# First layer of a two-layer encoder: a written TensorE order in small pieces, and softmax steps queued further back

## The chip, the cores and the metric

The kernel runs on one core of one Trainium2 chip. TensorE (PE) multiplies matrices into PSUM, VectorE (DVE) and ScalarE (ACT) read PSUM and SBUF, GpSimd (POOL) reads and writes SBUF alone, SyncE (SP) issues the DMAs. Each engine takes its instructions in their order; semaphores hold an instruction until what it reads is there. The metric is the device time of one execution in microseconds (us), lower is better.

## The reference, cut to what matters

1024 frames of a new stream and 32 frames of a running one go through two layers. Layer 0, the one that is changed, projects its normed input to u, q, k, v and two gates, and has two branches: trailing means of u over windows of 2, 4, 8 and 16 frames, mixed by a matrix per group (four groups of 128 channels), and attention of 8 heads over the frame's own chunk of 64 and the 8 before it.

```python
def even_mixer(h, w_in, w_mix, scale, table, w_out, pool_hist=None, k_hist=None, v_hist=None):
    proj = h @ w_in
    u, q, k, v, g_pool, g_att = jnp.split(proj, [P, P + A, P + 2 * A, P + 3 * A, 2 * P + 3 * A], axis=-1)
    ...
        pool_out = multi_scale_pool(u, 0, 0, w_mix, scale)
        att = band_attention_prompt(q, k, v, table)
    ...
    mixed = jnp.concatenate([pool_out * jax.nn.silu(g_pool),
                             att.reshape(B, L, A) * jax.nn.silu(g_att)], axis=-1)
    return mixed @ w_out, new_pool, new_k, new_v
```

In the attention, `s` is q times k plus a bias by distance, `p = softmax(s)`, and the output `p` times v. The 32 frames of the running stream ("the sample") attend to 512 cached rows and themselves. Layer 1 is not touched.

## The kernel before, in words

The 1056 tokens stand in the columns of all tiles, in three groups of 384, 384 and 288 (`GR`). A dense pass (`dense`, `mm3`) multiplies one 128-column block of a weight with the whole input: 8 slices of the input dimension, three products each (high by high part, low by high, high by low: L106, L107, L108) into a PSUM tile pd (three of them), which DVE or ACT empties (`scaled` L256, `gated` L268 and L271, u L612). A weight comes in two halves: SP loads wr, ACT rounds it to wh (L93), POOL subtracts to get wl (L94, "the split").

The loop goes over four pairs of heads. A pair has the dense passes K and GA (the gate, in the one tile ga), the attention of its two heads, and between its parts the passes of `PLAN`: v and q of the next pair, u and gp of a group of channels. Attention runs in two halves of 512 queries: scores in banks of PSUM (ps, three tiles), L342 and L343; bias and copy to SBUF tiles st (DVE L347, ACT L355, and a corner cleared by POOL, L359); maxima over the keys (DVE `mx` L371, then POOL's all-reduce over partitions `mb`, L373); subtraction (DVE L377), exponential (ACT L378); the product with the values, PV (L388); at the end of a half `att_out`: POOL multiplies by the gate (L408), DVE forms a reciprocal (L409) and multiplies (L410). There is one tile each of ro, rg and mb.

The sample has scores of its own (L429, L430) with a small all-reduce `smb` (L441) and an exponential (L444), its ten products with the values (L454), reciprocal and scaling (L456, L457) and a transpose back (L459). `pool_sums` forms the trailing sums of u: one sum on POOL (L477) per doubling of the window, four for group 3 down to one for group 0, then DVE corrects the first frames (L481) and updates u (L483). `pool_mix` multiplies by the group's matrix (PE L495) into one PSUM tile pm, which DVE empties (L497). After the loop `out_proj` reads what was stored, and POOL and DVE split it (L196).

Tile's scheduler orders all engines; the source order only ranks them.

Of the kernel before, what the change touches and what calls it, by code (L numbers as in the profile page):

```python
# [7 lines left out]
F32 = mybir.dt.float32  # L8
# [7 lines left out]
DEC = 32  # L16
# [17 lines left out]
class Net:  # L34
# [5 lines left out]
    # ---------------------------------------------------------------- consts  # L40
    def consts(self):
# [4 lines left out]
        # the table of the activations, before the data is there  # L46
# [24 lines left out]
    # keeps [s, t] with s <= t  # L71
# [4 lines left out]
    # ---------------------------------------------------------------- dense  # L76
# [40 lines left out]
    # the same, one token group at a time, to be put between other work; "make" gives evac when the tile starts  # L117
    def later(self, take, xs, make, after=None):
        box = {}

        def step(gi):
            if gi == 0:
                box["w"] = take()
                box["ev"] = make()
# [3 lines left out]
        self.fills += [lambda gi=gi: step(gi) for gi in range(3)]  # L128
# [15 lines left out]
    # r = 1/sqrt(sum/1024 + eps), on all partitions, from per-partition sums; worked out with the tokens on the partitions  # L144
# [44 lines left out]
    # split x * g into two parts of 12 bits  # L189
# [15 lines left out]
    # the input: one group's tokens, with tiles that are not in use yet for what comes in  # L205
# [23 lines left out]
    # ---------------------------------------------------------------- layer 0  # L229
# [21 lines left out]
    def scaled(self, dst, sc=None):  # L251
        nc, r = self.nc, self.r0

        def ev(gi, s, n, p):
            if sc is None:
                nc.vector.tensor_tensor(out=dst[:, s:s + n], in0=p[:, :n], in1=r[:, s:s + n], op=ALU.mult)  # L256
            else:
                nc.vector.scalar_tensor_tensor(out=dst[:, s:s + n], in0=p[:, :n], scalar=sc, in1=r[:, s:s + n],
                                               op0=ALU.mult, op1=ALU.mult)
        return ev  # L260

    # (1 + tanh(g/2)) * g, twice the silu
    def gated(self, dst):
        nc, r = self.nc, self.r0

        def ev(gi, s, n, p):
# [4 lines left out]
            nc.vector.scalar_tensor_tensor(out=d, in0=th[:, :n], scalar=1.0, in1=d, op0=ALU.add, op1=ALU.mult)  # L271
        return ev

    def v_tokens(self, vT, pr):
# [8 lines left out]
        for b0 in (0, 4, 8):  # L283
            p = self.pv.tile([128, 512], F32, name="pv") if b0 == 4 else self.pm.tile([128, 512], F32, name="pm")
            for b in range(b0, min(b0 + 4, NCH)):
                L = clen(b)
                q = p[:L, (b - b0) * 128:(b - b0) * 128 + 128]
                nc.tensor.transpose(q, vT[:, 128 * b:128 * b + L], self.ident)
                nc.scalar.mul(out=v4[:L, b, 0::2, :], in_=q.rearrange("p (t c) -> p t c", c=64), mul=self.rcol[:L, b:b + 1])
        for e in range(2):  # L290
            c0 = pr * 128 + e * 64
            cs = slice(e * 128, e * 128 + 64)
            nc.sync.dma_start(out=io["vo"][0:512, c0:c0 + 64].rearrange("(b p) c -> p b c", p=128), in_=vt[:, 4:8, cs])
            nc.sync.dma_start(out=io["vo"][512:544, c0:c0 + 64], in_=vt[:DEC, 8, cs])
        return vt

    # hi and lo of both heads, stacked on the partitions
# [21 lines left out]

    def att_s(self, pr, e, hf, Q, KA, KB, B):  # L320
# [7 lines left out]
        for group in banks:  # L328
            st = self.lp.tile([128, 1280], F32, name="st", bufs=4)
            tiles.append((st, [j for js in group for j in js]))  # L330
            off = 0
            for js in group:
# [3 lines left out]
                for j in js:  # L336
                    a, b = max(128 * j, q0), min(128 * j + 640, q1)
                    n = b - a
                    dst = st[:, off + w:off + w + n]
# [884 lines left out]
```

## Time and profile before

| | us |
|---|---|
| median of 3 runs | 1275.29 |
| the runs | 1273.09, 1277.02, 1275.29 |
| span of the profiled execution | 1273.6 |
| PE busy | 1200.1 (94%) |
| DVE busy | 688.7 (54%) |
| ACT busy | 471.5 (37%) |
| POOL busy | 316.3 (25%) |
| loop over the pairs of heads | 41.5 to 448.5 |
| mean granted TensorE clock | 0.973 |

The span runs from the first to the last instruction of one profiled execution; the median is of executions without a profile. [...]

### The profile page before, as it was taken

The numbers are of one execution on the slowest core, as the hardware profiler recorded it, in microseconds if no ns is written. First come the engines' busy times: TensorE is split into PE (matmuls) and PEld (weight loads), VectorE is DVE, ScalarE is ACT, GpSimd is POOL, SyncE is SP. The second block draws the span as 40 slices with busy tenths as digits, with TensorE's granted clock in tenths as the row PEclk, the third lists the DMA queues.
The fourth block names the chain that finished last, engine by engine and source line by source line (L and its number), as shares of the span: only waits on it lengthen the run. The fifth ranks groups of instructions, "written<-read, shape, count | busy, mean of one in ns | idle before, by whom it ended". The sixth has DMA issues, their size and how long they took to land.

```text
span 1273.6 us, 19526 instructions
## 1 busy us (share of the span) xinstructions
PE 1200.1 (94%) x7457; PEld 1148.3 (90%) x7457; DVE 688.7 (54%) x1457; ACT 471.5 (37%) x976; POOL 316.3 (25%) x409
## 2 busy tenths in 40 slices
PE   6998898978997979999999999999999999999996
PEld 6997797977897859999999989999999999998996
DVE  7654474564676644777435643574237532567324
ACT  6532333243443335543033423343224322346421
POOL 3222532342234223552010320021002210123232
PEclk9998988989999989999999989999999999999998
DMA  6311120111120225332111132113111311113323
GB/s 216 114 38 33 44 85 26 51 59 34 64 71 22 78 85 168 100 127 83 49 51 53 37 71 97 38 49 95 46 50 51 76 68 50 42 60 122 127 99 124
DMA packets 79613, 94.03 MB, mean 74 GB/s; under 512 B 19208, under 2 KB 56856, under 8 KB 79520
## 3 DMA queue, kind: packets, MB, share of 16 engines
q1 hardware_dynamic: 79520, 92.79, 23.5%
q8 instruction: 58, 0.95, 0.3%
q14 instruction: 35, 0.29, 0.1%
HBM read 72.64 MB, written 21.69 MB: 74 GB/s over the span
## 4 chain that ended last, share of the span: by engine, by line
PE 77%; DVE 6%; issue 5%; DMA 5%; POOL 3%; ACT 2%; SPq 0%; DVEq 0%; POOLq 0%; ACTq 0%
PE pd L107 20%; PE pd L106 20%; PE pd L108 20%; PE pv L388 3%; DMA xr<-mix 2%; PE pm L883 1%; PE ps L951 1%; PE ps L343 1%; PE ps L342 1%; POOL qT L477 1%; DMA wr<-in_w0o 1%; POOL wl L94 1%; PE pv L918 1%; DMA MA<-mdr 1%; PE pv L920 1%
## 5 line engine op out<-in xcount | busy, mean ns | idle before, releaser
L106 PE MATMUL pd<-xh,wh 128*128 128x384 f32 (+1 forms) x1864 | 613.6, 330 | 13.5 <-DVE ga L268 6.8
L107 PE MATMUL pd<-xl,wh 128*128 128x384 f32 (+1 forms) x1864 | 612.8, 329 | 13.9 <-POOL xl L196 9.5
L108 PE MATMUL pd<-xh,wl 128*128 128x384 f32 (+1 forms) x1864 | 612.7, 329 | 1.7 <-DVE wl L94 1.6
L107 PEld LDWEIGHTS pd<-xl,wh 128*128 128x128 f32 x1864 | 356.1, 191 | 19.1 <-POOL xl L196 10.2
L106 PEld LDWEIGHTS pd<-xh,wh 128*128 128x128 f32 x1864 | 356.2, 191 | 18.2 <-ACT wh L93 7.6
L108 PEld LDWEIGHTS pd<-xh,wl 128*128 128x128 f32 x1864 | 356.0, 191 | 5.2 <-DVE wl L94 3.0
L93 ACT CAST wh<-wr 128x512 fp32r<-128x512 f32 x158 | 91.4, 618 | 149.6 <-PE pd L107 122.4
L94 DVE TENSOR_TENSOR wl<-wr,wh 128x512 fp32r<-128x512 f32 x116 | 80.5, 718 | 23.7 <-ACT wh L93 22.1
L94 POOL TENSOR_TENSOR wl<-wr,wh 128x512 fp32r<-128x512 f32 x42 | 57.8, 1392 | 116.8 <-ACT wh L93 59.6
L187 POOL TENSOR_TENSOR acc<-acc,sqt 128x384 f32<-128x384 f32 (+1 forms) x48 | 56.6, 1178 | 92.2 <-ACT sqt L186 87.8
L388 PE MATMUL pv<-st,vt 128*128 128x512 f32 (+1 forms) x192 | 58.7, 448 | 0.2 <-ACT st L378 0.2
L73 POOL TENSOR_SCALAR_AFFINE_SELECT D<-D 128x128 f32<-128x128 f32 (+1 forms) x36 | 11.9, 331 | 180.8 <-ACT D L947 168.1
L388 PEld LDWEIGHTS pv<-st,vt 128*128 128x128 f32 x192 | 36.2, 195 | 20.7 <-issue 12.4
L963 POOL TENSOR_TENSOR qa<-qT,MA 128x128 f32<-128x128 f32 (+1 forms) x64 | 27.1, 441 | 107.1 <-DMA MA<-mdr 68.4
L965 POOL TENSOR_TENSOR qal<-qa,qah 128x256 fp32r<-128x256 f32 (+1 forms) x32 | 27.0, 847 | 103.9 <-ACT qah L964 91.6
L347 DVE TENSOR_TENSOR st<-ps,B 128x256 f32<-128x256 f32 (+1 forms) x72 | 26.1, 377 | 45.0 <-PE ps L343 44.4
L377 DVE TENSOR_TENSOR st<-st,mb 128x512 f32<-128x512 f32 (+1 forms) x96 | 40.0, 485 | 15.7 <-POOL mb L373 14.1
L256 DVE TENSOR_TENSOR row<-pd,r 128x384 f32<-128x384 f32 (+1 forms) x36 | 18.6, 521 | 54.4 <-PE pd L108 54.2
L983 DVE SCALAR_TENSOR_TENSOR C<-C,MA,ps 128x258 f32<-128x258 f32 x64 | 30.4, 478 | 32.2 <-PE ps L920 19.0
L373 POOL PARTITION_ALL_REDUCE mb<-mx x16 | 28.8, 1799 | 66.5 <-issue 25.2
L378 ACT ACTIVATE st<-st 128x1280 f32<-128x1280 f32 x24 | 30.4, 1272 | 31.2 <-DVE st L377 31.1
L355 ACT ACTIVATE st<-ps,far 128x256 f32<-128x256 f32 (+3 forms) x56 | 25.6, 487 | 38.9 <-DVE st L347 35.8
(306 smaller groups left out, 1675.8 us busy)
## 6 DMA issues: line engine op xcount, KB each, us to landing
wr<-in_w SPq DMA_DIRECT2D x128, 256.0 KB, 2.7
xr<-mix SPq DMA_DIRECT2D x26, 192.0 KB, 2.9
wr<-in_w0o SPq DMA_DIRECT2D x16, 256.0 KB, 3.1
MA<-mdr SPq DMA_DIRECT2D x32, 128.0 KB, 3.2
wr<-in_w1o SPq DMA_DIRECT2D x16, 256.0 KB, 3.2
x<-in_x SPq DMA_DIRECT2D x16, 192.0 KB, 2.8
x<-x1d SPq DMA_DIRECT2D x16, 192.0 KB, 3.8
out_y<-y SPq DMA_DIRECT2D x16, 192.0 KB, 2.1
```

The source lines that it names most:

```text
L93: nc.scalar.copy(out=wh[:, k], in_=wr)
L94: eng.tensor_tensor(out=wl[:, k], in0=wr, in1=wh[:, k].bitcast(F32), op=ALU.subtract)
L106: nc.tensor.matmul(out=p, lhsT=wh[:, k], rhs=xh[:, k], start=first and i == 0, stop=False)
L107: nc.tensor.matmul(out=p, lhsT=wh[:, k], rhs=xl[:, k], start=False, stop=False)
L108: nc.tensor.matmul(out=p, lhsT=wl[:, k], rhs=xh[:, k], start=False, stop=last and i == len(ks) - 1)
L187: (eng or nc.gpsimd).tensor_tensor(out=acc, in0=acc, in1=t[:, :n], op=ALU.add)
L373: nc.gpsimd.partition_all_reduce(mb, mx, 128, bass_isa.ReduceOp.max)
L377: nc.vector.tensor_tensor(out=dst, in0=dst, in1=mb[:, a - q0:b - q0], op=ALU.subtract)
L378: nc.scalar.activation(out=st, in_=st, func=AF.Exp)
L388: nc.tensor.matmul(out=pv[:, a - q0:b - q0], lhsT=vt[:, j, 64 * e:64 * e + 128], rhs=dst, start=(i == 0), stop=(i == len(order) - 1))
L963: nc.gpsimd.tensor_tensor(out=qa[:, d, :L], in0=qT[:, d, t], in1=Ab, op=ALU.mult)
L983: nc.vector.scalar_tensor_tensor(out=Cn[:, d], in0=C[:, d], scalar=Ab[:, L - 1:L], in1=pu, op0=ALU.mult, op1=ALU.add)
```

## The change

The loop's body becomes `pair`, inside `tc.manual_schedule` for PE alone: PE's order is the source order, that of all other engines is still the scheduler's. A dense pass is cut into 24 pieces of three products (`later(fine=True)`), and `along` puts other steps in at given piece numbers. In `PLAN` v goes last. The scores are cut into banks, with all products of a bank ahead of its emptying (`v_tokens` likewise). Softmax is split: `soft` (maxima) right after the last bank, `power` (subtraction, exponential) 20 or 22 pieces later and, on DVE, behind the emptying of the last dense tile (`issue_after(self.ev)`). PV of the first half stands at pieces 42 and 50 (36 and 44 in the last pair), that of the second half in the next pair's K and GA passes. The sample's scores run in the GA pass; its values are at piece 62, its turn at 67. Mixing is queued by `due`. There are two tiles mb, and the sample's five subtractions become one. The sum of PE's products stays. Lines move: L373 becomes L410, L377 L418, L378 L420, L408 to L410 L456 to L458, L429 L479, L454 L511, L456 and L457 L514 and L515, L459 L521, L477 L539, L481 and L483 L543 and L545, L495 and L497 L557 and L559, L268 L288, L347 L382, L359 L394.

```diff
-PLAN = ((("v", 1), ("q", 1), ("u", 3), ("gp", 3)), (("v", 2), ("q", 2), ("u", 2)), (("v", 3), ("q", 3), ("gp", 2)),
+
+PLAN = ((("q", 1), ("u", 3), ("gp", 3), ("v", 1)), (("q", 2), ("u", 2), ("v", 2)), (("q", 3), ("gp", 2), ("v", 3)),
         (("u", 1), ("gp", 1), ("u", 0), ("gp", 0)))
...
+        def piece(gi, k):
+            s, n = GR[gi]
+            if k == 0:
+                if gi == 0:
+                    begin()
+                box["p"] = self.pd.tile([128, 512], F32, name="pd")
+            self.mm3(box["p"][:, :n], box["w"], xs[gi], [k], k == 0, k == 7)
+            if k == 7:
+                box["ev"](gi, s, n, box["p"])
+                if gi == 2 and after is not None:
+                    after()
+        if fine:
+            self.fills += [lambda gi=gi, k=k: piece(gi, k) for gi in range(3) for k in range(8)]
...
-        mb = self.lp.tile([128, 512], F32, name="mb", bufs=1)
...
+            mb = self.lp.tile([128, 512], F32, name="mb", bufs=2)
+            nc.gpsimd.partition_all_reduce(mb, mx, 128, bass_isa.ReduceOp.max)
+            return mb
...
+        def power(mb):
+            with self.tc.issue_after(self.ev):
+                for st, js in tiles:
+                    for j in js:
+                        dst, a, b = place[j]
+                        nc.vector.tensor_tensor(out=dst, in0=dst, in1=mb[:, a - q0:b - q0], op=ALU.subtract)
+            for st, js in tiles:
+                nc.scalar.activation(out=st, in_=st, func=AF.Exp)
+        box = {}
+
+        def step(b, i):
+            scores(banks[b], i)
+            if b == len(banks) - 1 and i == 2:
+                box["mb"] = soft()
+        return place, [lambda b=b, i=i: step(b, i) for b in range(len(banks)) for i in range(3)], lambda: power(box["mb"])
...
-            for b in range(5):
-                nc.vector.tensor_tensor(out=ss[:, b], in0=ss[:, b], in1=mb, op=ALU.subtract)
+            box["ss"], box["mb"] = ss, mb
+        def power():
+            ss, mb = box["ss"], box["mb"]
+            with self.tc.issue_after(self.ev):
+                nc.vector.tensor_tensor(out=ss, in0=ss, in1=mb.unsqueeze(1).to_broadcast([128, 5, 2, DEC]), op=ALU.subtract)
-            # token-major
+        def values():
+            ss, vt = box["ss"], own["vt"]
+            for e in range(2):
...
+    def along(self, events, n=999):
+        events = sorted(events, key=lambda e: e[0])
+        i = 0
+        while i < n and self.fills:
+            while events and events[0][0] <= i:
+                events.pop(0)[1]()
+            self.fill()
+            i += 1
+            for d in self.due:
+                d[0] -= 1
+            while self.due and self.due[0][0] < 0:
+                self.due.pop(0)[1]()
+        for e in events:
+            e[1]()
+    def pair(self, pr, take, xs, rows, do, before, Kc, GA):
+        nc = self.nc
+        box = {}
+        def make_k():
+            box["kT"] = self.row()
+            return self.scaled(box["kT"])
+        def make_ga():
+            box["gate"] = self.lp.tile([128, T], F32, name="ga", bufs=1)
+            return self.gated(box["gate"])
+        qT = rows["q", pr]
+        Q = self.stacked(qT, "qa")
+        self.later(lambda: take(Kc + pr), xs, make_k, fine=True)
+        before, pvs = before
+        self.along(before + [(8, f) for f in pvs[:1]])
+        kT = box["kT"]
+        nc.sync.dma_start(out=self.io["ko"][128 * pr:128 * pr + 128], in_=kT[:, 512:T])
+        KA = self.stacked(kT, "ka")
+        KB = self.swapped(KA, "kb")
+        B = self.lp.tile([128, 2, 256], F32, name="B", bufs=1)
+        for e in range(2):
+            src = self.ext[2 * pr + e, 0:1, 128:129]
+            nc.sync.dma_start(out=B[:, e], in_=bass.AP(tensor=src.tensor, offset=src.offset, ap=[[383, 128], [1, 256]]))
+        nc.gpsimd.memset(B[64:128, :, 0:64], NEG)
+        self.later(lambda: take(GA + pr), xs, make_ga, fine=True)
+        ev = [(14, f) for f in pvs[1:]]
+        def values():
+            box["vt"], turn = self.v_tokens(rows["v", pr], pr)
+            box["turn"] = turn
+            turn(0)
+        s_scores, s_power, s_values = self.att_sample(pr, qT, kT, box, B)
+        ev += [(4, s_scores), (17, values), (20, lambda: box["turn"](4))]
+        self.along(ev)
+        gate, vt = box["gate"], box["vt"]
+        for f, g in PLAN[pr]:
+            do[f](g)
+        n = len(self.fills)
+        end = pr == NPAIR - 1
+        place, ev, more = {}, [], []
+        for e, hf, at in ((0, 0, 1), (1, 0, 8), (0, 1, 16), (1, 1, 46 if end else 54)):
+            place[e, hf], steps, power = self.att_s(pr, e, hf, Q, KA, KB, B)
+            ev += [(at + 2 * i, f) for i, f in enumerate(steps)]
+            late = (at + 2 * len(steps) + (20 if hf == 0 else 22), power)
+            (more if hf == 1 and e == 1 and not end else ev).append(late)
+        ev += [(4, lambda: box["turn"](8)), (2, s_power)]
+        od = {}
+        def pv(e, hf):
+            if e == 0:
+                od[hf] = self.att_new()
+            self.att_pv(e, hf, place[e, hf], vt, od[hf])
+            if e == 1:
+                self.att_out(pr, od[hf], 512 * hf, 512 * hf + 512, gate)
+        ev += [(36 if end else 42, lambda: pv(0, 0)), (44 if end else 50, lambda: pv(1, 0))]
+        ev += [(62 + 5 * i, f) for i, f in enumerate(s_values)]
+        if end:
+            ev += [(72, lambda: pv(0, 1)), (95, lambda: pv(1, 1))]
+        self.along(ev + [m for m in more if m[0] < n], n)
+        more = [(m[0] - n, m[1]) for m in more if m[0] >= n]
+        return more, [lambda: pv(0, 1), lambda: pv(1, 1)]
...
+                       lambda: self.due.extend([(0, 6, 20, 20)[g] + 4 * i * (g > 0), f] for i, f in
+                                               enumerate(self.pool_mix(g, pools["u", g], pools["gp", g]))), True)
...
+        with tc.manual_schedule(engines={mybir.EngineType.PE}):
+            for pr in range(NPAIR):
+                last = self.pair(pr, take, xs, rows, do, last, Kc, GA)
+            while self.due:
+                self.due.pop(0)[1]()
```

The order of instructions shows where the other engines' work now stands. On POOL a row "ISA" that names no tile stands ahead of each all-reduce that follows ordinary work, and ahead of the ordinary work that follows an all-reduce; there are 27 in the program before and 35 after.

The first place is POOL between the second pair and its neighbours, where a pair's last product with its gate stands, after which the tile ga can be written anew (ro is that product, vt the clearing of the tile of values, wl a weight's split, mb and smb all-reduces, qT the sums of u). Before, from the second pair to the third:

```order
L477 TENSOR_TENSOR qT<-qT 128x1083
L94 TENSOR_TENSOR wl<-wr,wh 128x512
L477 TENSOR_TENSOR qT<-qT 128x1079
L94 TENSOR_TENSOR wl<-wr,wh 128x512
L277 MEMSET vt 128x13x64
L408 TENSOR_TENSOR ro<-ro,ga 128x512
L94 TENSOR_TENSOR wl<-wr,wh 128x512 x2
L373 ISA
L373 ISA mb<-mx 128x512
```

After, from the first pair to the second:

```order
L491 ISA smb<-sm 128x64
L297 MEMSET vt 128x13x64
L456 ISA
L456 TENSOR_TENSOR ro<-ro,ga 128x512
L94 TENSOR_TENSOR wl<-wr,wh 128x512 x2
L410 ISA
L410 ISA mb<-mx 128x512 x2
```

Before, the clear and the gate product follow sums and splits with no change of kind between; now a small all-reduce stands ahead of them, and an ISA row between the clear and the product.

The second place is POOL in the middle of the second pair, around the sums of u. Before (the other two sums are those quoted above):

```order
L94 ISA
L94 TENSOR_TENSOR wl<-wr,wh 128x512 x2
L432 MEMSET ss 128x64
L408 TENSOR_TENSOR ro<-ro,ga 128x512
L359 MEMSET st 64x64 x4
L94 TENSOR_TENSOR wl<-wr,wh 128x512
L642 MEMSET B 64x2x64
L94 TENSOR_TENSOR wl<-wr,wh 128x512
L477 TENSOR_TENSOR qT<-u 128x1085
L373 ISA
L373 ISA mb<-mx 128x512
L477 ISA
```

After:

```order
L94 ISA
L94 TENSOR_TENSOR wl<-wr,wh 128x512 x2
L410 ISA
L410 ISA mb<-mx 128x512
L94 ISA
L94 TENSOR_TENSOR wl<-wr,wh 128x512
L539 TENSOR_TENSOR qT<-u 128x1085
L94 TENSOR_TENSOR wl<-wr,wh 128x512
L456 TENSOR_TENSOR ro<-ro,ga 128x512
L539 TENSOR_TENSOR qT<-qT 128x1083
L394 MEMSET st 64x64 x4
L539 TENSOR_TENSOR qT<-qT 128x1079
```

The three sums now follow one another behind the third all-reduce, with splits and the first half's gate product between, and the corners of the next half's scores are cleared (st) between the second and third sum.

The third place is DVE in the second pair, around the sample's reciprocals (srec) and scaling (so), which PE's transpose of the sample's output waits for. Before:

```order
L258 SCALAR_TENSOR_TENSOR row<-pd,r 128x288
L456 RECIPROCAL srec<-pv 32x1
L423 COPY qd<-row 64x32 x2
L457 TENSOR_SCALAR so<-pv,srec 32x64
L306 TENSOR_TENSOR qa_2269<-row,qa_2269 64x1024
L612 TENSOR_TENSOR u<-pd,r 128x384
L461 TENSOR_TENSOR smo<-ps,ga 128x32
```

After:

```order
L408 TENSOR_TENSOR mx<-mx,st 128x384
L543 TENSOR_TENSOR qT<-qT,cnt 128x7
L545 SCALAR_TENSOR_TENSOR u<-qT,u 128x32
L514 RECIPROCAL srec<-pv 32x1
L408 TENSOR_TENSOR mx<-mx,st 128x256
L545 SCALAR_TENSOR_TENSOR u<-qT,u 128x1024
L515 TENSOR_SCALAR so<-pv,srec 32x64
L514 RECIPROCAL srec<-pv 32x1
L408 TENSOR_TENSOR mx<-mx,st 128x128
L408 TENSOR_TENSOR mx<-mx,st 128x384
L382 TENSOR_TENSOR st<-ps,B 128x256
L515 TENSOR_SCALAR so<-pv,srec 32x64
```

The sample's four instructions now stand behind the correction of the sums (qT, cnt), which reads the last of them, and the update of u stands between them. In the last pair, DVE has `ro<-ro,rg` of the first half (L458), two emptyings, eight subtractions (L418) and a maximum ahead of the first emptying of pm (L559).

## Rows read from the trace of the kernel before

**Rows 1.** The head of the profile's page.

```profile
span 1273.6 us, 19526 instructions
```

**Rows 2.** Waits of PE, 41 to 470 us: total, times, longest.

```profile
PE pv L454 <- ACT ss L444: 20.4, 4, 6.1
PE pd L107 <- POOL xl L196: 9.5, 1, 9.5
PE pd L106 <- DVE ga L268: 6.8, 1, 6.8
PE pm L495 <- DVE u L483: 6.5, 2, 5.5
```

**Rows 3.** Windows: busy time (entries) of each engine, PE's clock, DMA.

```profile
41.50:448.50 407.00, 373.06 (x2152) 343.97 (x2152) 240.19 (x464) 149.73 (x262) 127.64 (x127) 0.95 0.17 52
101.60:107.90 6.30, 6.30 (x29) 5.96 (x30) 3.06 (x9) 1.34 (x4) 1.78 (x1) 0.50 0.00 0
```

**Rows 4.** Timeline of POOL: start, length, what, [idle before <- ended by].

```profile
90.57 2.53 POOL L94 TENSOR_TENSOR wl<-wr,wh 128x512 fp32r<-128x512 f32 x2 [6.91 <-ACT ss L435]
99.60 0.54 POOL L441 PARTITION_ALL_REDUCE smb<-sm  x1 [6.41 <-issue]
...
223.84 3.51 POOL L94 TENSOR_TENSOR wl<-wr,wh 128x512 fp32r<-128x512 f32 x2 [7.05 <-ACT st L378]
```

**Rows 5.** Timeline of POOL, second pair.

```profile
254.21 1.80 POOL L373 PARTITION_ALL_REDUCE mb<-mx  x1 [6.00 <-PE pd L108]
...
262.99 2.37 POOL L477 TENSOR_TENSOR qT<-qT 128x1083 f32<-128x1083 f32 x1 [6.97 <-issue]
...
270.51 1.80 POOL L408 TENSOR_TENSOR ro<-ro,ga 128x512 f32<-128x512 f32 x1
```

**Rows 6.** Timeline of DVE, the same time.

```profile
256.05 3.31 DVE L377 TENSOR_TENSOR st<-st,mb 128x128 f32<-128x128 f32 x8 [4.82 <-POOL mb L373]
...
268.59 1.24 DVE L481 TENSOR_TENSOR qT<-qT,cnt 128x7 f32<-128x7 f32 x1 [5.08 <-POOL qT L477]
...
274.14 3.35 DVE L409 RECIPROCAL rg<-rg 128x512 f32<-128x512 f32 x1
277.41 0.95 DVE L268 TENSOR_TENSOR ga<-pd,r 128x384 f32<-128x384 f32 x2
```

**Rows 7.** Groups of POOL, 41.5 to 460 us: busy, mean ns | idle before.

```profile
L94 POOL TENSOR_TENSOR wl<-wr,wh 128x512 fp32r<-128x512 f32 x42 | 57.8, 1392 | 116.8 <-ACT wh L93 59.6 <-ACT ss L435 21.1 <-ACT st L378 14.3
L373 POOL PARTITION_ALL_REDUCE mb<-mx x16 | 28.8, 1799 | 66.5 <-issue 25.2 <-DVE mx L371 20.4 <-DVE st L347 6.4
L477 POOL TENSOR_TENSOR qT<-qT 128x1083 f32<-128x1083 f32 (+2 forms) x6 | 13.4, 2228 | 13.8 <-issue 13.8
L408 POOL TENSOR_TENSOR ro<-ro,ga 128x512 f32<-128x512 f32 x7 | 10.4, 1489 | 15.9 <-ACT ro L396 15.9
L277 POOL MEMSET vt<- 128x832 f32 x3 | 2.4, 786 | 0.0
```

**Rows 8.** Timeline of PE, the same time as rows 5.

```profile
258.00 0.33 PE L107 MATMUL pd<-xl,wh 128*128 128x384 f32 x1
258.17 0.33 PE L108 MATMUL pd<-xh,wl 128*128 128x384 f32 x1
259.39 4.47 PE L388 MATMUL pv<-st,vt 128*128 128x512 f32 x16
...
269.71 0.39 PE L342 MATMUL ps<-qa,kb 128*128 128x512 f32 x1
269.94 0.39 PE L343 MATMUL ps<-qa,ka 128*128 128x512 f32 x1
```

**Rows 9.** Timeline of PE, the sample's values in the first pair.

```profile
101.56 1.42 PE L454 MATMUL pv<-vt,ss 128*32 128x65 f32 x10 [4.30 <-ACT ss L444]
```

**Rows 10.** Groups of DVE by shape, 41.5 to 460 us.

```profile
L371 DVE TENSOR_TENSOR mx<-mx,st 128x256 f32<-128x256 f32 x24 | 13.6, 565 | 0.7
L483 DVE SCALAR_TENSOR_TENSOR u<-qT,u 128x1024 f32<-128x1024 f32 x4 | 5.8, 1459 | 0.0
```

More of the change, by code (lines that the diff above doesn't have):

```diff
@@ L115, in dense, with later, begin @@
             evac(gi, s, n, p)
-    def later(self, take, xs, make, after=None):
+    def later(self, take, xs, make, after=None, fine=False):
         box = {}
+        def begin():
+            box["w"] = take()
+            box["ev"] = make()
         def step(gi):
             if gi == 0:
-                box["w"] = take()
-                box["ev"] = make()
+                begin()
             self.dense(box["w"], xs, box["ev"], (gi,))
@@ L282, in v_tokens, with turn @@
         v4 = vt.rearrange("p b (t c) -> p b t c", c=64)
-        for b0 in (0, 4, 8):
+        def turn(b0):
             p = self.pv.tile([128, 512], F32, name="pv") if b0 == 4 else self.pm.tile([128, 512], F32, name="pm")
@@ L327, in att_s, with scores @@
         banks = (((0,), (1, 3), (2,)),) if hf == 0 else (((0, 2), (3,), (1,)), ((4,), (5, 7), (6,)))
[L328 to L332, printed above, removed]
+        off = 0
+        def scores(group, i):
+            nonlocal off
+            if i == 0:
+                tiles.append((self.lp.tile([128, 1280], F32, name="st", bufs=4), [j for js in group for j in js]))
+                off = 0
+            st = tiles[-1][0]
+            for js in group[i:i + 1]:
                 p = self.ps.tile([128, 512], F32, name="ps")
@@ L412, in att_out, with att_sample @@
         nc.sync.dma_start(out=self.mix[r0:r0 + 128, q0:q1], in_=o[:, :n])
-    def att_sample(self, pr, qT, kT, vt, B, gate):
+    def att_sample(self, pr, qT, kT, own, B):
         nc, io = self.nc, self.io
@@ L457, in rest, with turn @@
                 nc.vector.tensor_scalar(out=o[:, e], in0=pv[:, e, v0:v0 + 64], scalar1=rec[:, e:e + 1], scalar2=None, op0=ALU.mult)
+            box["o"] = o
+        def turn():
+            o, gate = box["o"], own["gate"]
             p = self.ps.tile([128, 512], F32, name="ps")
@@ L462, in rest @@
             nc.sync.dma_start(out=self.mix[512 + 128 * pr:640 + 128 * pr, SEQ:T], in_=mo)
-        return rest
+        return scores, power, (values, turn)
     def pool_sums(self, g, u):
@@ L489, in pool_mix, with piece @@
         nc.sync.dma_start(out=wm, in_=io["wmix"][g])
-        for s, n in GR:
+        def piece(s, n):
             p = self.pm.tile([128, 512], F32, name="pm")
@@ L590, in make @@
                 return self.plain(rows["v", pr])
-            self.later(lambda: take(Vc + pr), xs, make)
+            self.later(lambda: take(Vc + pr), xs, make, fine=True)
         def do_q(pr):
@@ L596, in make @@
                 return self.scaled(rows["q", pr], 0.125)
-            self.later(lambda: take(Qc + pr), xs, make)
+            self.later(lambda: take(Qc + pr), xs, make, fine=True)
         def do_u(g):
@@ L619, in after @@
                 self.pool_sums(g, u)
-            self.later(lambda: take(U + g), xs, make, after)
+            self.later(lambda: take(U + g), xs, make, after, True)
         def do_gp(g):
```

113 lines of the change are left out of this document (44 added, 69 removed).

## The prediction

> **What bounds the kernel now.** I read the totals first: TensorE (PE) is busy for 94% of a span of 1273.6 us [rows 1], so time can only be won where it stands still or runs slowly. PE's waits in the first layer (41 to 470 us) are few and long: four times the ten small products of the sample's values wait for the exponential of its scores, 20.4 us together; the first product after the gate's dense pass waits once for VectorE (DVE) to empty a PSUM tile, 6.8; the mixing products wait for the finished u, 6.5; the output projection waits for GpSimd's (POOL) split, 9.5 [rows 2]. That is 43.2 us. [...] A mean of 0.95 over 407 us, made of 1.0 and 0.5, is 41 us at half speed, which cost half of themselves, 20 us; a part lies in the idle time already counted, and I take 2.6 us for each of the seven stretches (the one at the output projection with them), 18 us. So 61 us is all that an order of PE can win: 1214 us is the floor.
>
> Then I asked what is late in each wait, and it is not DVE's own work. POOL stands still for 6 to 7 us whenever it changes between all-reduces (softmax maxima) and ordinary arithmetic: 6.41 and 6.00 us ahead of an all-reduce, 6.91 and 6.97 us ahead of the next split or sum; where the view finds nothing that it waits for it says "issue" [rows 4, 5]. I use 6.2 and 7.0. What such a change does further on is seen at 256 to 278 us: an all-reduce ends at 256.0, POOL's next sum starts at 263.0, DVE stands at the correction of that sum until 268.6, and behind it in DVE's queue are the reciprocal (3.35 us) and the emptying of the gate's tile, which starts at 277.4; that is PE's 6.8 us [rows 2, 5, 6].
>
> **The change, part by part.** No product is added or left out, so PE's busy time stays. What changes is who stands ahead of whom.
>
> *Changes of kind on POOL.* POOL has six per pair of heads before and eight after: the order shows a row "ISA" without a tile at each, 27 in the program before and 35 after. Eight more at 6.2 or 7.0 are 53 us of POOL. For the second pair POOL has after the change 4 × (6.2 + 7.0) = 52.8, four wide all-reduces at 1.8 and a small one, 7.7, ten weight splits at 1.39, 13.9, three sums at 2.1 to 2.2, 6.5, two gate products at 1.49, 3.0 [rows 4, 5, 7], and some 3 of clearing: 87 us. PE's products of the same pair, from one K to the next, are 82 us by the spacings below. POOL becomes the longer queue; before, with two changes fewer, it had 74.
>
> [...]
>
> *PE's own pace*, to see how long it can run before it needs POOL. Two products of 384 columns start 0.17 us apart, so a piece (three of them) takes 0.52, and one of 288 columns 0.39 by its columns; a score product of 512 columns takes 0.23; PV of one head over the second half of the tokens, 2560 columns, 4.2 (16 entries, 4.47 less the last one's tail), over the first half, 1280 columns, 2.1; the sample's values 1.4 [rows 8, 9].
>
> *The sample's turn, pairs one to three.* POOL's queue meets PE at the third bank of the third score pass, 20 pieces into the plan: it clears a corner of what was emptied from that bank. The turn of the sample's values is at piece 67. Between them PE has 32 wide and 15 narrow pieces (22.5), 3840 columns of scores, two products each (3.45), two PV (4.2) and the sample's values (1.4): 31.6 us. POOL in that time has, in the second pair, a change (7.0), two splits (2.8), a change (6.2), an all-reduce (1.8), a change (7.0), a split, a sum, a split, the gate product and a sum (1.4 + 2.1 + 1.4 + 1.5 + 2.2), four clears (0.6) and a last sum (2.2): 36.2, begun 0.9 after the bank, as the clear waits for ScalarE's copy. DVE stands at the correction of the last sum meanwhile, and behind it are the update of u (1.46), three maxima at about 0.57, an emptying and the sample's own five short ones: 4.4 [rows 7, 10]. PE waits 36.2 + 0.9 + 4.4 − 31.6 = **10 us**. In the first pair a list of the same length starts 1.5 later, behind two all-reduces, and DVE's tail is 0.6 shorter: **10.8**. In the third pair there are no sums, but a second split: 29.7 + 0.9 + 5.0 − 31.6 = **4**. Before, DVE had the sample's reciprocal ahead of the corrections, and these turns cost nothing; the four waits for the exponential (20.4) go away, since the sample's scores now run in the gate's pass.
>
> *The gate's tile, pairs two to four.* There is one tile "ga", so the next gate can be written only after POOL's last product with the old one. After the change that product stands behind the last PV of the old pair, a clear (0.8) and a change (7.0), and takes 1.5; DVE then empties in 0.5: 9.8 us. PE has two wide and eight narrow pieces (4.2) and eight transposes of 128 columns, 0.21 each by the columns of PV: 5.9 us. It waits **3.9 us, three times, 11.8**, where it waited once, 6.8.
>
> *The mixing in the last pair.* DVE's reciprocal and product (L458) of the first half wait for POOL's gate product, at the end of a change, a sum, two splits, a sum, a change, an all-reduce, a change: 7.0 + 2.1 + 2.8 + 2.2 + 6.2 + 1.8 + 7.0 + 1.5 = 30.6, plus 0.9. Behind it on DVE are two emptyings, eight subtractions (3.31 us), a maximum and the emptying of the one mixing tile: 6.2 [rows 6, 7, 10]. PE has 27 wide and 12 narrow pieces, the same scores, two PV and one mixing product (0.6 by its columns), 27 us: it waits **11 us**. Before, the two waits for mixing were 5.5 in the first pair and 1.0 here [rows 2]; in the first pair the one tile now costs 1.5.
>
> *The end.* POOL's last change, sum and splits come out in several short waits of the projection and the last PV, **5 us** together, for 9.5.
>
> *At nothing:* the emptying after all products of a PSUM tile (three ps tiles, and the next pieces of dense work cover it), the second "mb", one subtraction for five, the moved PV and transposes: their exponentials are 2 to 8 us early by the same reckoning. If that cover went, each would cost its exponential, 1.3 us.
>
> Sum of PE's waits after: 10 + 10.8 + 4 + 11.8 + 11 + 1.5 + 5 = 54, against 43.2: +11. Long ones are seven as before (two of 10, three of 3.9, one of 4, one of 11), and the clock's 18 us stays; should the four short ones not bring the clock down, it is 4 × 2.6 = 10 less, and I take 2 off for that. The profiled execution is 1273.6 in span, the median 1275.3, so 1.7 lies around it: 1273.6 + 1.7 + 11 − 2 = **1284 us**. The bounds: the clock holds at the four and each of the seven waits is a little shorter, 1274; each is 2 longer, 1297.
>
> **The rivals.** (1) *POOL's changes run beside other work*, so that a chain has half of them: 10 less in each long chain, 3.5 in the gate's. All waits but the end's go, and seven stretches at half speed with them: 1284 − 10 − 10.8 − 4 − 11 − 3 × 3.5 = 1238, and less by up to 18 of clock: 1220 to 1238. It decides as soon as POOL's chain between bank and turn is under 31 us instead of 37. For it: the plan puts 20 pieces between maxima and subtraction, and POOL is busy for only 128 us of the loop's 407 [rows 3]. Against it: each time the 6 to 7 us lie behind a finished instruction [rows 4, 5]. (2) *One wait for another*: POOL gets ahead while PE goes at half speed, so that the waits come to 43 again: 1275. For it: of a stretch of 6 us at 0.50, POOL gains 3 each time [rows 3]; I have counted that nowhere. (3) *DVE and POOL slow each other*: the subtractions and maxima, now in one block behind the dense evictions, run against POOL's two-input work. Two splits took 2.53 us in one place and 3.51 in another, the gate product 1.80 against a mean of 1.49 [rows 4, 5, 7]. A quarter more on the 13 us of such work in a chain is 3, in each of four: 1296.
>
> [...]
>
> **How the numbers follow.** A change within 0.3% (3.8 us) can't be told from none. Forecast 1284: 0.50 (of it slower 0.41, within 0.04, faster 0.05); rival 1: 0.22, all faster; rival 2: 0.16, within; rival 3: 0.12, slower. Faster 0.27, same 0.20, slower 0.53. The range leaves out most of rival 1 (its time can lie anywhere from 1220 to the forecast's lower bound, as more or less of a change is hidden) and the far end of rival 3: 1243 to 1298; the forecast's own is 1274 to 1297.
>
> **What would show it.** Right: PE's waits named by so (L515) for ps (L521), ga (L288) for pd, gp (L559) for pm, of 10, 4 and 11 us; none for the sample's exponential; 6 to 7 us of POOL ahead of 32 changes in the loop. Wrong: PE's waits in the loop under 25 us together, or POOL's changes shorter where its queue is full; or scores waiting for a ps tile, which I took to be covered.

## The result, and the profile after

The changed kernel takes 1289.95 us (median of 4 runs, 1289.24 to 1292.64), the kernel before 1274.88 (4 runs, 1273.09 to 1277.02): 1.0121 times as long, with a 95% interval of 1.0102 to 1.0141. The profiled executions differ alike, 1287.9 against 1273.6 us in span [rows 1].

The head of the page, and the engines' line on it (PE is TensorE):

```profile
span 1287.9 us, 19531 instructions
PE 1205.5 (94%) x7457; PEld 1152.4 (89%) x7457; DVE 685.9 (53%) x1441; ACT 471.9 (37%) x976; POOL 312.2 (24%) x409
```

The head of PE's waits from 41 to 490 us (us in total, times, longest), which answer to [rows 2]:

```profile
PE pd L106 <- DVE ga L288: 15.0, 3, 5.1
PE ps L521 <- DVE so L515: 10.3, 2, 8.4
PE ps L521 <- DVE qT L543: 9.7, 1, 9.7
PE pm L557 <- DVE gp L559: 8.7, 2, 6.1
PE pv L436 <- ACT rg L445: 3.7, 1, 3.7
...
PE pd L107 <- POOL xl L215: 0.5, 1, 0.5
PE ps L372 <- ACT st L390: 0.2, 1, 0.2
```

None of the 20.4 us for the sample's exponential is left, and 9.5 at the output projection have become 0.5. In their place PE waits for the sample's turn (so, qT), the gate's tile (ga), the mixing (gp) and once ahead of PV (rg). All rows of the view sum to 51.7, where those of before came to 43.4.

Windows, with the columns of [rows 3]: the loop, a stretch behind a wait of 9.65 us, one behind 2.56, one behind 1.82, and the rest of the program.

```profile
41.50:464.00 422.50, 373.83 (x2137) 344.81 (x2137) 237.67 (x445) 148.21 (x258) 125.66 (x128) 0.94 0.16 49
125.20:131.00 5.80, 5.80 (x22) 5.74 (x23) 4.97 (x11) 1.48 (x3) 1.23 (x2) 0.50 0.18 48
...
145.00:148.00 3.00, 3.00 (x7) 2.39 (x8) 0.62 (x1) 2.07 (x4) 0.00 (x0) 0.50 0.21 69
344.00:350.00 6.00, 6.00 (x32) 5.33 (x31) 1.70 (x3) 1.15 (x3) 1.24 (x2) 1.00 0.32 105
...
486.20:1287.90 801.70, 781.83 (x5069) 763.78 (x5067) 401.88 (x912) 285.94 (x643) 167.40 (x226) 0.99 0.25 77
```

The last row holds the last 5069 products. The last 5068 of before are in this window of it:

```profile
476.00:1273.60 797.60, 778.57 (x5068) 761.13 (x5066) 403.26 (x912) 285.56 (x642) 168.15 (x226) 0.99 0.25 78
```

So the same products begin 10.2 us later, and the part from there on takes 4.1 more: not all of the 14.3 us lie in the first layer. Ahead of that point PE stands still for 62.6 us instead of 54.5 (486.20 less its busy 423.64, against 476.00 less 421.55), and is busy for 2.1 more.

The sample's turn in the second pair shows how such a wait comes about. GpSimd (POOL) from the clear of the score tile to the last sum (start, length, what, idle before and what ended it), to be held against [rows 5]:

```profile
204.25 0.14 POOL L394 MEMSET st<- 64x64 f32 x1 [0.45 <-ACT st L390]
211.67 3.05 POOL L94 TENSOR_TENSOR wl<-wr,wh 128x512 fp32r<-128x512 f32 x2 [7.28 <-issue]
220.75 1.80 POOL L410 PARTITION_ALL_REDUCE mb<-mx  x1 [6.02 <-DVE u L756]
229.77 1.30 POOL L94 TENSOR_TENSOR wl<-wr,wh 128x512 fp32r<-128x512 f32 x1 [7.22 <-ACT row L267]
231.03 1.99 POOL L539 TENSOR_TENSOR qT<-u 128x1085 f32<-128x1085 f32 x1
...
234.21 1.28 POOL L456 TENSOR_TENSOR ro<-ro,ga 128x512 f32<-128x512 f32 x1
...
237.75 2.08 POOL L539 TENSOR_TENSOR qT<-qT 128x1079 f32<-128x1079 f32 x1
```

VectorE (DVE) in the same time, where [rows 6] showed the correction ahead of the reciprocal:

```profile
235.52 2.47 DVE L458 TENSOR_TENSOR ro<-ro,rg 128x512 f32<-128x512 f32 x1 [5.13 <-POOL ro L456]
...
241.30 0.15 DVE L543 TENSOR_TENSOR qT<-qT,cnt 128x7 f32<-128x7 f32 x1
...
244.27 0.26 DVE L515 TENSOR_SCALAR so<-pv,srec 32x64 f32<-32x64 f32 x1
```

And PE, whose products take 0.44 us behind the wait (granted clock 0.50 from 245 to 250) where they took 0.29 ahead of it (1.00 from 234 to 236):

```profile
235.94 0.30 PE L108 MATMUL pd<-xh,wl 128*128 128x288 f32 x1
244.68 0.28 PE L521 MATMUL ps<-ident,so 32*128 32x32 f32 x1 [8.44 <-DVE so L515]
...
245.30 0.44 PE L107 MATMUL pd<-xl,wh 128*128 128x288 f32 x1
```

In the 35.4 us from 204.39 to 239.83 POOL stands still three times for 6.0 to 7.3 us; the work between is gapless. DVE loses 5.13 us to the gate product, which ends at 235.49, comes to the correction 1.5 us after the last sum, and has the sample's scaling done at 244.53; PE's transpose follows at 244.68. So the transpose waits for the gate product and for 9.2 us of DVE behind it, not for the last sum.

### The profile page after: what moved, and what is told of

Same layout as the page of the kernel before. It is cut to its first block, busy times and chain, and to the rows that moved or that the text cites. A ratio compares the mean times of both kernels' runs of the same rounds, so it can differ in the third digit from the quotient of the medians.

```text
span 1287.9 us, 19531 instructions
## 1 busy us (share of the span) xinstructions
PE 1205.5 (94%) x7457; PEld 1152.4 (89%) x7457; DVE 685.9 (53%) x1441; ACT 471.9 (37%) x976; POOL 312.2 (24%) x409
## 4 chain that ended last, share of the span: by engine, by line
PE 75%; DVE 10%; DMA 5%; ACT 4%; issue 3%; POOL 3%; SPq 0%; DVEq 0%; ACTq 0%; POOLq 0%
PE pd L106 20%; PE pd L107 19%; PE pd L108 19%; PE pv L436 4%; DMA wr<-in_w0o 2%; DMA xr<-mix 2%; DVE st L418 1%; PE pm L1001 1%; DVE xl L221 1%; PE ps L1069 1%; PE ps L373 1%; PE pv L1036 1%; PE ps L372 1%; DMA MA<-mdr 1%; PE pv L1038 1%
## 5 line engine op out<-in xcount | busy, mean ns | idle before, releaser
L418 DVE TENSOR_TENSOR st<-st,mb 128x512 f32<-128x512 f32 (+1 forms) x96 | 47.6, 561 | 14.7 <-POOL mb L410 14.7
L420 ACT ACTIVATE st<-st 128x1280 f32<-128x1280 f32 x24 | 30.4, 1271 | 51.4 <-DVE st L418 43.5
L410 POOL PARTITION_ALL_REDUCE mb<-mx x16 | 28.8, 1804 | 82.2 <-DVE mx L408 26.8
L457 DVE RECIPROCAL rg<-rg 128x512 f32<-128x512 f32 x8 | 26.8, 3351 | 23.1 <-ACT rg L445 23.1
```

What stands on the lines that cost most here:

```text
L410: nc.gpsimd.partition_all_reduce(mb, mx, 128, bass_isa.ReduceOp.max)
L418: nc.vector.tensor_tensor(out=dst, in0=dst, in1=mb[:, a - q0:b - q0], op=ALU.subtract)
L420: nc.scalar.activation(out=st, in_=st, func=AF.Exp)
```

## The experiments

**Theory:** POOL's changes of kind (between all-reduces and ordinary work) make these waits, in both kernels; eight more of them in the change cost what the moved waits win. **Rivals:** the written PE order costs time by itself, whatever POOL does; or only the place of the sample's turn does.

**1 and 2. The all-reduces taken out.** The maxima stay each partition's own (copied, so the softmax has other numbers); three changes of kind are left in the program. The edit in the changed kernel, and likewise in the one before:

```diff
-            nc.gpsimd.partition_all_reduce(mb, mx, 128, bass_isa.ReduceOp.max)
+            nc.gpsimd.tensor_copy(out=mb, in_=mx)
...
-            nc.gpsimd.partition_all_reduce(mb, m, 128, bass_isa.ReduceOp.max)
+            nc.gpsimd.tensor_copy(out=mb, in_=m)
```

> The changed kernel with the 20 all-reduces over partitions of the first layer replaced by a plain copy on POOL (the maximum over the keys of a partition stands in for the maximum over all keys, so the softmax is left incomplete). POOL then never changes its kind of work in the loop: 3 of the 35 changes are left. Theory (POOL's changes of 6 to 7 us make PE's waits): the waits fall from 52 us to under 15 and most of the half clock goes, 1225 to 1245 us. Rival A (the written PE order costs time of itself, since nothing can slide into a wait): the waits stay at other places, over 1270. Rival B (DVE's queue is late by its own work and by sharing with POOL): the waits at so, ga and gp shrink by less than half, about 1260 to 1270.

> The same replacement in the kernel before (softmax left incomplete in the same way), 3 of 27 changes left. Theory: before, too, its waits are POOL's changes, so 43 us of waits fall to under 15: 1225 to 1245, and the changed kernel without changes (the run beside it) is at least as fast, within 5 us or below. Rival A: this one stays well below the changed kernel's time by more than 10 us. If the changes matter for neither, 1270 to 1275.

The changed kernel took 1237.43 us (ratio to the kernel before 0.9704, interval 0.9659 to 0.9748), the kernel before 1226.52 (0.9613, 0.9572 to 0.9655). So 52 us of the one and 49 of the other hang on the changes of kind and the all-reduces with them. Without them the written order is still 11 us behind: PE waits for the turn (3.8 and 2.2), for PV (2.9) and in smaller places, about 16 us together, against 6 in the order of before. The theory had the changed kernel at least as fast here; more than 10 us behind was the mark of the rival that the written order costs time by itself.

One thing has to be kept in mind for these two and the later runs. In the changed kernel PE's order stays as written under these edits: its products stand in the same order in the traces of runs 1, 6 and 7, and all but three, at 47 us, in 3 and 5. In the kernel before the scheduler orders PE anew: in runs 2, 4 and 9 between a third and a half of the first layer's products stand elsewhere. So the gains of those three are of the edit and a new PE order together.

**3 and 4. The all-reduces kept, ordinary work taken off POOL.** Splits, sums and gate products run on DVE, so five changes are left in the changed kernel and seven in the one before; what is computed stays the same:

```diff
-        nc.gpsimd.tensor_tensor(out=o[:, :n], in0=o[:, :n], in1=gate[:, q0:q1], op=ALU.mult)
+        nc.vector.tensor_tensor(out=o[:, :n], in0=o[:, :n], in1=gate[:, q0:q1], op=ALU.mult)
...
-            nc.gpsimd.tensor_tensor(out=dst[:, lo:L], in0=src[:, lo:L], in1=src[:, lo - sh:L - sh], op=ALU.add)
+            nc.vector.tensor_tensor(out=dst[:, lo:L], in0=src[:, lo:L], in1=src[:, lo - sh:L - sh], op=ALU.add)
...
-        self.weng = nc.gpsimd
+        self.weng = nc.vector
```

> The changed kernel with POOL's ordinary arithmetic of the loop on DVE: 42 weight splits, 10 sums of u, 8 gate products. The result stays whole. POOL keeps all-reduces and clears, 5 of 35 changes are left. DVE gets some 30 + 12 + 5 = 47 us more on 238 in a loop of 422. Theory: waits named so, ga and gp go to under 15 us, 1230 to 1250. Rival B (DVE is the late engine): its queue grows by a fifth, the waits stay or grow, 1285 or more. Rival A: about 1275 to 1290.

> The same move in the kernel before, 7 of 27 changes left. Theory: its 43 us of waits fall to some 15 to 20, 1240 to 1258. Rival B: DVE later than before, 1275 or more. The changed kernel with the same move (the run beside it) should lie at or below this one by the theory, above it by rival A.

The changed kernel took 1232.61 us (0.9664, 0.9622 to 0.9706), the kernel before 1238.41 (0.9711, 0.9661 to 0.9761), 2 us under what was expected. The all-reduces as such cost little (1232.61 us with them for 1237.43 in run 1 without, 1238.41 for 1226.52 in the kernel before): it is their mixture with other work that does. Of the kernel before, 8.7 us of the rest lie at the output projection, where an all-reduce and a split on POOL still stand next to each other:

```profile
PE pd L107 <- POOL xl L196: 8.7, 1, 8.7
```

**5 to 7. One kind of ordinary work at a time, in the changed kernel.** The third hunk above alone (splits; 21 changes left), the second alone (sums; 35 left), the first alone (gate products; 35 left).

> The changed kernel with its 42 weight splits of the layer on DVE, all else on POOL as it was: 21 of the 35 changes are left. Theory, place by place: the sample's turns lose their waits (POOL's list between bank and turn falls from 36 us to about 17, PE has 31.6); the gate's tile keeps its three waits, since a small all-reduce still stands ahead of the clear and the product, 4 to 5 us each; the mixing in the last pair keeps 6 to 8. Waits about 25 for 52: 1250 to 1260 us. If not the changes but POOL's sum of work counts, the gate's waits shrink as well: 1240. Rival B (30 us more on DVE make it late): 1280 or more.

> The changed kernel with the 10 sums of u on DVE instead of POOL; all 35 changes stay. Theory: only the 2.1 to 2.2 us of each sum leave the list, so the sample's turns in the first two pairs keep about 4 of 10 and 8 us, the mixing in the last pair 3 to 5 of 6, the gate's waits stay at 5 each: waits 36 to 42, 1270 to 1280 us. If the sums and not the changes are what is late, the two turns fall to nothing: under 1265.

> The changed kernel with the 8 gate products on DVE; all 35 changes stay, but none of them stands between the last PV of a pair and the next gate. Theory: the three waits at ga (15 us with their clock, some 20) go, the sample's turns lose 1.5 each, the mixing in the last pair 1 to 3: 1262 to 1272 us. If the waits only move on (POOL is the longer queue over a whole pair, so that what is won at ga is lost at the next turn), the turns grow by what the gate loses: 1283 to 1290.

Splits: 1264.74 us (0.9908, 0.9886 to 0.993). Sums: 1273.02 (0.9983, 0.9957 to 1.0009; its ten runs lie between 1268.08 and 1283.73). Gate products: 1260.18 (0.9871, 0.9849 to 0.9894). The first is 5 us over the range expected: the turns, which were to lose their waits, kept 9.2 us, while the gate's tile kept its three (16.0), as expected. The last is 2 under its range. From 1289.95 these are gains of 25, 17 and 30 us, 72 together, where all three at once gave 57: the chains share their links. The last says most, since it takes no change of kind away: it takes the product with the gate from behind them. PE's wait for ga (15.0) is gone, while those for the turn, 20.0 by their two rows in the changed kernel (so and qT), stay at 18.1; they did not grow by what the gate lost:

```profile
PE ps L521 <- DVE so L515: 18.1, 3, 9.9
PE pm L557 <- DVE gp L559: 8.3, 3, 4.9
```

So what the changes of kind cost here hung on what stood behind them and who waited for that, not on their number alone: with 35 of them the changed kernel took 1289.95 us, and 1260.18 in run 7. With the sums on DVE the turns still waited (15.0): in the second pair POOL's gate product ended at 230.0, behind its third change of kind, DVE stood at L458 until then, and the transpose started at 236.14. The sums were not needed to hold it, though they lengthen it: their absence takes the turns from 20.0 to 15.0.

**8 and 9. The best of each order.** In both, the edits of 3 and 4, and the first group's splits of the output projection on DVE; in the changed kernel the sample's turn is later as well:

```diff
-                    self.split_x(x, k, src, None, nc.gpsimd if gi < 2 and k % 2 == 0 else None)
+                    self.split_x(x, k, src, None, nc.gpsimd if gi == 1 and k % 2 == 0 else None)
...
-        ev += [(62 + 5 * i, f) for i, f in enumerate(s_values)]
+        ev += [(54 + 16 * i, f) for i, f in enumerate(s_values)]
```

> The changed kernel with splits, sums and gate products on DVE (as in the run that had 1232.6), the sample's values at piece 54 and its turn at piece 70 instead of 62 and 67, and the output projection's splits for the first token group on DVE too. The two waits left at the sample's turn (7.7 us) should go, with one or two stretches of half clock: 1220 to 1228 us. If DVE's own queue is by now what the turn waits for, the wait moves with the turn: 1230 to 1235.

> The kernel before, with weight splits, rotary sums and gate products on VectorE and the first group's split of the output projection on VectorE as well (the second group keeps GpSimd); the all-reduces stay. Same result. It is the run of the kernel before with ordinary work on VectorE (1238.4 us) without the 8.7 us that TensorE waited there for GpSimd's split at the output projection. Theory (the changes of kind are the cost, the order of TensorE is worth little once they are gone): 1226 to 1231, within 5 us of the changed kernel in the same form (1225.6). Rival (the written order is itself worth more): the 8.7 us come back elsewhere and it stays at 1235 or over.

The written order: **1225.56 us** (0.9596, 0.9577 to 0.9614). The scheduler's own order: 1227.88 (0.9638, 0.9615 to 0.966). Either beats both kernels by 4%; what the written order adds is 2 us of it by the medians, with runs that overlap (1224.27 to 1227.75 and 1225.06 to 1231.67), and 0.4% by the ratios, each taken to its own runs of the kernel before. All of PE's waits from 41 to 490 us in the faster one:

```profile
PE pd L108 <- DVE wl L94: 1.8, 1, 1.8
PE pm L175 <- POOL acc L206: 1.4, 1, 1.4
PE pv L436 <- ACT st L420: 1.1, 1, 1.1
PE pm L557 <- DVE gp L559: 0.7, 1, 0.7
```

**10. Only the sample's turn moved.** The last hunk above alone; 35 changes stay.

> The changed kernel, with the three entries of the sample's values and its turn at pieces 54, 70 and 86 of the plan in place of 62, 67 and 72; GpSimd's work and its 35 changes of kind stay. Same result. Prediction's reckoning: each turn has a few pieces more of TensorE's work ahead of it, so the waits of 9.65 and 8.44 us for the turn shrink by 1 to 3 us each and the 1.82 goes: 1280 to 1286. Theory (GpSimd's list is the longer queue of the pair, so what one place gives another takes): the wait for the gate's tile and for the mixing grow by as much, 1286 to 1292. If the place of the turn alone were the cost, 1270 or below.

It took 1288.47 us (1.011, 1.0079 to 1.014), as the changed kernel. The waits for the turn are gone, but those for the mixing grew from 8.7 to 14.7, and new ones came at the scores (st) and the sample's values (rg):

```profile
PE pd L106 <- DVE ga L288: 15.0, 3, 5.3
PE pm L557 <- DVE gp L559: 14.7, 3, 8.3
PE ps L372 <- ACT st L390: 4.7, 2, 4.5
PE pv L511 <- ACT rg L445: 4.5, 2, 3.5
```

The place of the turn is not the cause. What one place gives back is for the most part lost at the next (PE's waits sum to 48.0, for 51.7), as the longer queue would have it; the gate's tile did not take its share, as I had expected it to.

**11. Eight more changes of kind in the kernel before, TensorE's order left alone.**

```diff
+        tiny = self.cp.tile([128, 1], F32, name=f"tiny{pr}")
+        nc.gpsimd.partition_all_reduce(tiny, vt[:, 0, 64:65], 128, bass_isa.ReduceOp.max)
```

> The kernel before, with TensorE's order left as it is, and one small all-reduce over a 128x1 tile more in each pair, read by nothing, so that GpSimd has 35 changes of kind in place of 27. Same result. Theory (the eight more changes are what the changed kernel pays): slower, 1282 to 1296, with new waits of 6 us or more for GpSimd's next ordinary work. Rival (only where TensorE's order puts its waiters decides, GpSimd has slack): 1275 within 3 us.

It took 1303.78 us (1.0229, 1.021 to 1.0248), more than either theory said. The two largest waits of the whole execution:

```profile
PE pv L456 <- ACT ss L446: 26.5, 4, 8.7
PE pd L106 <- ACT xh L199: 12.3, 1, 12.3
```

The second does not belong to the loop: the first pair's added all-reduce landed at 12.8 us, ahead of the sums of squares of the input, and POOL stood still 8.83 us before and 8.61 us behind it. Without those 12.3 the span is 13.6 us over that of before, for the six changes of the other pairs. All of PE's products stand in the same order in both traces, so no new PE order is in this. That more changes alone slow this order is borne out, at about the size of the change's own loss, but not as cleanly as meant.

**12. The changed kernel with PE's order left to the scheduler again.**

```diff
-        with tc.manual_schedule(engines={mybir.EngineType.PE}):
+        with nullcontext():
```

> The changed kernel, with TensorE's instructions put in order by the scheduler again instead of as written; the pieces, the emptying after all products, the softmax steps further back and GpSimd's 35 changes stay. Same result. Theory (the changes of kind are the cost): 1280 to 1292, the waits in other places. Rival (the written order of TensorE is the cost): 1275 or below.

It took 1262.61 us (0.9916, 0.9883 to 0.9948), with all 35 changes of kind. Against my theory: it is 27 us faster than the written order and 12 faster than before. The head of PE's waits:

```profile
PE pd L106 <- DVE ga L288: 10.4, 3, 3.5
PE ps L521 <- DVE qT L543: 6.9, 1, 6.9
PE ps L521 <- DVE so L515: 4.6, 1, 4.6
```

The same waits, shorter; the mixing has 2.9 of 8.7. The second pair's turn on PE shows a part of how:

```profile
234.72 0.34 PE L106 MATMUL pd<-xh,wh 128*128 128x384 f32 x1
...
238.54 0.34 PE L107 MATMUL pd<-xl,wh 128*128 128x384 f32 x1
243.48 0.28 PE L521 MATMUL ps<-ident,so 32*128 32x32 f32 x1 [4.60 <-DVE so L515]
```

The transpose is ready at about the same time (243.5 against 244.7), but all narrow pieces of the dense pass and most of the eight wide ones of the next (234.72 to 238.9) run ahead of it, where the written order had five narrow pieces and that next pass still behind it. The other engines' order moved with this edit too (in each of the first two pairs POOL's first gate product now stands behind the second sum, not ahead of it), so not all of the 27 us need be PE's own order; the two weren't separated.

Taken together, the theory holds in half. POOL's changes of kind make the lateness: with PE's order as written, 52 to 57 us go without them or without ordinary work between them (runs 1 and 3), and in the kernel before 47 to 49, a new PE order included (runs 2 and 9). But how much of it becomes waits hangs on the order: 35 changes take 1289.95 us with the written one and 1262.61 with the scheduler's. So the rival on the written order is right too, by up to 27 us, as long as POOL is late. With POOL's chains gone the written order is anything from 11 us behind the scheduler's (runs 1 and 2) to 6 ahead (3 and 4), and 2 ahead in the best form of each (8 and 9).

## Why the prediction was right, and where it was off

The forecast of 1284 was 6 us low; 1289.95 lies in its range and in the likeliest case's own (1274 to 1297). By its terms:

- **The turns** (10.8, 10 and 4) were 9.65, 8.44 and 1.82. In the second pair POOL's list took 35.4 us for the 36.2 reckoned, and the tail from its end to the transpose 4.85 for 4.4. But the path was another. What I had put down to DVE's stand at the correction began earlier, at L458; the correction itself came late but did not wait, and in the first pair it stands behind the sample's scaling (124.98 against 124.78 us). POOL's list up to the gate product is 31.1 us in the second pair, 4.3 shorter than to the last sum, and DVE's way from there to the transpose 9.2, 4.3 longer than the 4.85: that the terms come so near is luck in part.
- **The gate's tile** (11.8) was 15.0. From the start of the clear to PE's product behind the write there are 10.0 us, for 9.8 reckoned; PE's cover was 5.0 us, not 5.9. The rows between the second pair and the third:

```profile
279.72 0.80 POOL L297 MEMSET vt<- 128x832 f32 x1 [2.28 <-PE pv L436]
287.79 1.25 POOL L456 TENSOR_TENSOR ro<-ro,ga 128x512 f32<-128x512 f32 x1 [7.28 <-issue]
289.08 1.02 DVE L288 TENSOR_TENSOR ga<-pd,r 128x384 f32<-128x384 f32 x2 [4.81 <-POOL ro L456]
289.69 0.69 PE L106 MATMUL pd<-xh,wh 128*128 128x384 f32 x1 [4.94 <-DVE ga L288]
```

- **The mixing** (11 in the last pair, 1.5 in the first) was 6.10 and 2.56. The last pair's term is nearly whole if the wait just ahead of it is added, 3.74 at PV, which delayed PE by as much.
- **"At nothing"** failed there: the moved PV of the second head was to find its exponential early. It didn't, for reasons in the last section. Nor had the sum the 1.2 us that the sample's scores wait for kn in the second pair.
- **The end** (5) was 2.9: 1.0, 0.7 and 0.5 in the projection, at xh, wl and xl, and 0.7 ahead of the last PV.
- **The clock** (2 less) was 1 more: busy time weighted with one minus the granted clock, in windows of 1 us, comes to 18.1 us from 41 to 490 before and 19.4 after. I had counted seven stretches at half speed, 2.6 us each by an estimate from the loop's mean granted clock [rows 3], and thought that some might go; there are nine, 2.2 each.
- **The rest of the program** is what the sum missed. It had nothing for what follows the first layer, and that takes 4.1 us more, in a part that the diff doesn't touch; 2.9 of it are the clock's by the same reckoning (5.8 against 2.9), and 0.8 is idle time. Why is open.

The sum of PE's waits in the layer was 51.7 for 54, the layer 10.2 us longer for the 9 that I had with the clock; the 4.1 behind it make the most of the 6 us between forecast and median. The nearness of the sum is luck in part as well: the turns, the mixing and the end were put 10.8 us too high together, the gate's tile, PV, kn and the scores 8.3 too low.

Of the rivals, the first (changes hidden beside other work) is refuted by the idle times at the 32 changes of kind in the loop, 5.8 to 7.9 us each and no shorter where the queue is full. The second (waits of 43 again) isn't borne out: 51.7. The third (DVE and POOL slow each other) was real for DVE, ahead of PV in the last pair and in the turns. From the end of POOL's gate product to the transpose DVE took 9.9 and 9.2 us in the first two pairs, where POOL goes on with sums, and 5.1 in the third, where it has only clears. L458 alone took 2.47 in the first two, for 0.69 in the third. By an estimate from these rows, less the work that the third pair doesn't have, 3 to 4 us of each of the two waits are of this kind, where I had priced 3 and left it out of the sum. The cover of the three ps tiles held, 0.2 us; in run 10 it did not, 4.7.

The two prices of a change, 6.2 us ahead of an all-reduce and 7.0 ahead of other work, held: the trace has 6.02 ahead of the all-reduce above and 7.22 and 7.28 ahead of the splits, and over the 32 changes in the loop the means are 6.25 and 7.20.

## What to carry to other kernels

Look at the slack engine's queue before the bound engine's order: an engine with a 24% busy share made nearly every long wait here, since each switch between two kinds of its work cost 5.8 to 7.9 us in which it did nothing. Moving the ordinary work to an engine that had the room won 3%, and 4% with a part of the projection's splits moved as well, with either order of TensorE; the best order around the switches won 1%. Where a producer's lateness can't be removed, an order that is written out needs ready work placed between it and its reader, or should stay with the scheduler, which here could put a dense slice ahead of a late transpose.

## What the runs showed of the hardware

**DVE stretched beside POOL.** In the last pair POOL has a sum, two splits and a sum without a gap, and DVE maxima, an emptying and subtractions. Of POOL:

```profile
407.36 1.99 POOL L539 TENSOR_TENSOR qT<-u 128x1085 f32<-128x1085 f32 x1 [6.98 <-PE pd L108]
409.32 2.73 POOL L94 TENSOR_TENSOR wl<-wr,wh 128x512 fp32r<-128x512 f32 x2
412.02 2.31 POOL L539 TENSOR_TENSOR qT<-qT 128x1083 f32<-128x1083 f32 x1
```

Of DVE, and of ScalarE and PE behind it:

```profile
407.54 3.36 DVE L408 TENSOR_TENSOR mx<-mx,st 128x256 f32<-128x256 f32 x2
...
412.39 3.48 DVE L418 TENSOR_TENSOR st<-st,mb 128x512 f32<-128x512 f32 x4
...
415.97 1.27 ACT L420 ACTIVATE st<-st 128x1280 f32<-128x1280 f32 x1 [7.78 <-DVE qT L543]
...
418.35 3.85 PE L436 MATMUL pv<-st,vt 128*128 128x512 f32 x8 [3.74 <-ACT rg L445]
```

Two maxima of 128x256 took 3.36 us; in run 8, where POOL has no such work, the group's mean is 0.420 each, so these took four times as long:

```profile
L408 DVE TENSOR_TENSOR mx<-mx,st 128x256 f32<-128x256 f32 x24 | 10.1, 420 | 0.3
L458 DVE TENSOR_TENSOR ro<-ro,rg 128x512 f32<-128x512 f32 x8 | 5.5, 683 | 0.0
```

The four subtractions took 3.48 us, where the same four took 1.70 there. That is 2.5 and 1.8 us, over 4 together, ahead of the exponential. PV waited 3.74 for it and for ScalarE's two copies out of the one tile pv (L444, L445), which stood behind it and ended at 418.30. The second line is the product L458, 2.47 us beside POOL's sums in the first two pairs. I had allowed a quarter more, and DVE's instructions stretched by far more than POOL's: the three POOL rows above took 1.99, 2.73 and 2.31 us, and the shortest of the same shape in the layer 1.99, 2.51 and 1.98. By which mechanism DVE is held up, no run shows.

**The clock and short waits.** Behind a wait of 1.82 us at 340.7 the granted clock stayed at 1.00 (344 to 350); behind one of 2.56 at 144.96 it was 0.50 (145 to 148), as it was behind every wait of 3.7 us or more in the loop. The length of a wait alone does not tell it: behind two of 1.00 and 0.73 us close together (467.41 and 468.58) it was 0.50 from 470 to 472, and behind one of 1.31 (519.50) from 521 to 523.
